# A hybrid decoder layer on one core: the merge gates' products moved to a stage of their own with seven block products for eight, and the tiles of the attention's scores re-cut

## The chip, the core and the metric

One core of a Trainium2 chip runs the whole layer in one launch. The time is the device time of one execution in microseconds; less is better. Three runs of the kernel before took 1770.57 to 1776.94 us, with a median of 1774.29.

## What is computed

2048 tokens of width 1024, float32. With `h = x @ W_in + b_in` cut into columns:

```python
y_a = mla_attention(c_q, c_kv, k_pe, ...) * silu(z_a)      # 8 heads, 96-wide q and k, 64-wide v, causal
y_b = u_gelu * mixed(layer_norm(gelu(v))) * silu(z_b)      # 128x128 mixing per group of 64 columns
merged = sigmoid(g_a) * (y_a @ w_oa) + sigmoid(g_b) * (y_b @ w_ob)
out = layer_norm(alpha * x + merged @ w_out)
```

`g_a` and `g_b` are the merge gates: 1024 columns of `h` each, so 2048 of the 4640 columns of `W_in`. The columns `z_a`, `u` and `z_b` are 512 each.

## The kernel before

**Arithmetic.** Every float32 operand of a product is cut into a head `hi` and a rest `lo` (`split`, line 64: a copy on ScalarE, a subtraction on VectorE), and `mm3` (line 68) adds `hi*hi + hi*lo + lo*hi` in PSUM: three matmuls of up to 512 columns.

**Stages.** Stage 1 (lines 141 to 359) computes q, k and v of the attention and writes them to DRAM. Stage 2 (lines 361 to 491) computes v of the gating unit and mixes it: `gelu_v` per token tile, `mix` per chunk of 512 tokens, whose results `mo` go to DRAM (line 475). `gates()` (lines 493 to 568) makes the columns `u`, `z_b`, `z_a` and both merge gates: 28 blocks of 128 columns, for the chunks of x in two pairs, (0, 1) and then (2, 3), since two chunks of x fit on chip as (hi, lo). One block of one chunk is a `group`: 8 steps of three matmuls in one PSUM bank (pool `p3G`, two banks), then a bias on VectorE (line 522), or for the merge gates a tanh on ScalarE (line 518), and a store by GpSimd's queue (lines 519, 548). Line 571 runs 48 steps of this generator, next to the end of stage 2; the others fill the attention.

**The attention** (lines 574 to 767) handles 64 blocks (head, 256 queries). A block has three kinds of steps on TensorE. `score` (line 619) multiplies 128 queries with up to 512 keys into one bank of `ps_s` (four banks); VectorE adds the mask and takes the maximum (lines 631 to 639), and once the whole row has its maximum, ScalarE takes the exponentials (line 642). `turn` (line 648) transposes 2 x 2 blocks of probabilities into `ps_t` (one bank), which ScalarE and VectorE split into `ph` and `pl`. `product` (line 670) multiplies these with V.

**The order on TensorE** is written out ahead of time by a planner (lines 694 to 754) that keeps a clock `now` and assumes lags: a score tile's bank comes free `LAG_S` after the row plus `LAG_E` a tile, `ph` and `pl` are there `LAG_H` and `LAG_T` after a turn, the output bank `LAG_O` after a block. In each round it first pays back credit with one filler step of the gates, then tries a product, a turn, a score, and if none is due takes a filler step too. Every attention step adds `FILL` times its cost to the credit; a filler step is reckoned at 648 ns. What is left of the filler runs behind the attention (line 765). `tc.keep_in_program_order` fixes this order where `keep[0]` is set; elsewhere a scheduler orders each engine's instructions.

**The last stage** (lines 774 to 873) reads gates, attention and mixed v back, multiplies with `w_oa`, `w_ob` and `w_out`, and normalises.

SBUF pools opened in a stage's `ExitStack` are given back at its end, and the next stage's tiles lie in the same memory.

## Time and profile before

| what | before |
|---|---|
| median of three runs | 1774.29 us |
| lowest, highest run | 1770.57, 1776.94 us |
| profiled execution, first to last instruction | 1775.5 us |
| TensorE busy | 1731.4 us, 98% |
| VectorE busy | 1094.2 us, 62% |
| ScalarE busy | 754.6 us, 43% |
| GpSimd busy | 134.3 us, 8% |
| mean granted clock of TensorE | 0.992 |

The profiled execution's own time is known as its span, 1775.5 us, which lies within the runs. Times in the trace count from the first instruction. A matmul's row gives its start and how long it is in the pipeline; the next one starts before it ends, so what a matmul occupies is the distance between starts. Engines are PE (TensorE), PEld (its weight loads), DVE (VectorE), ACT (ScalarE), POOL (GpSimd) and SP (the queue of most DMAs).

### The profile page before, as it was taken

The page shows a single profiled execution, that of the slowest core. Times are in us where ns is not written, and L with a number is a line of the kernel's source. Part 1 is how long each engine was busy: PE and PEld are TensorE (multiplying, and loading weights), DVE is VectorE, ACT ScalarE, POOL GpSimd, SP SyncE. Part 2 cuts the span into 40 slices and gives each one's busy share as a digit, 9 for nine tenths or more (in the row PEclk, how much of TensorE's full clock was granted, in tenths as well). Part 3 has the DMA queues.
Part 4 walks back from the last instruction along what each step waited for, and adds up shares of the span by engine and source line. Part 5 has one row for each costly group of instructions (what it writes and reads, how often), then busy time and mean ns, then how long its engine had stood idle before and what let it go on. Part 6 is the DMA issues. An engine that isn't in the chain of part 4 may idle for free.

```text
span 1775.5 us, 25048 instructions
## 1 busy us (share of the span) xinstructions
PE 1731.4 (98%) x9249; PEld 1484.1 (84%) x9249; DVE 1094.2 (62%) x2209; ACT 754.6 (43%) x1708; POOL 134.3 (8%) x231
## 2 busy tenths in 40 slices
PE   7999999899999999999999999999999999999998
PEld 7999887788888888888788888888888877888886
DVE  6765686476664555444776666654445478777664
ACT  6533442255544454545655445544544341303020
POOL 0000011100000100000100000100001000000000
PEclk9999999999999999999999999999999999999999
DMA  6564851631321422422713212321123886657341
GB/s 220 194 196 160 276 170 38 181 99 49 101 72 66 140 68 66 119 68 75 215 62 89 76 55 81 122 72 59 60 66 120 283 270 225 215 197 215 120 131 72
DMA packets 111100, 229.06 MB, mean 129 GB/s; under 512 B 13120, under 2 KB 41920, under 8 KB 108608
## 3 DMA queue, kind: packets, MB, share of 16 engines
q1 hardware_dynamic: 99968, 193.88, 34.9%
q0 software_dynamic: 11008, 33.57, 5.4%
q8 instruction: 73, 1.20, 0.3%
q14 instruction: 51, 0.42, 0.1%
HBM read 155.50 MB, written 71.89 MB: 128 GB/s over the span
## 4 chain that ended last, share of the span: by engine, by line
PE 45%; issue 41%; DMA 5%; POOL 4%; DVE 3%; ACT 2%; SPq 0%; POOLq 0%; DVEq 0%; ACTq 0%
PE po L86 11%; PE psg L86 9%; PE psa L86 4%; PE psl L86 4%; PE pb L86 4%; PE pa L86 4%; PE pss L86 3%; PE pt L658 2%; POOL gd L519 2%; DMA wost<-in_w_out_dram 1%; PE psq L86 1%; POOL otd L686 1%; DMA xst<-in_xT_dram 1%; DMA mxd<-mo 1%; PE psr L86 1%
## 5 line engine op out<-in xcount | busy, mean ns | idle before, releaser
L86 PE MATMUL psg<-xh,fwh 128*128 128x512 f32 x896 | 375.3, 419 | 4.9 <-DVE fo L522 4.9
L66 DVE TENSOR_TENSOR pl<-pt,ph 128x512 fp32r<-128x512 f32 (+2 forms) x352 | 199.7, 567 | 287.2 <-ACT ph L65 285.5
L86 PE MATMUL psg<-xl,fwh 128*128 128x512 f32 x896 | 354.5, 396 | 0.0
L86 PE MATMUL psg<-xh,fwl 128*128 128x512 f32 x896 | 354.1, 395 | 0.0
L65 ACT CAST ph<-pt 128x512 fp32r<-128x512 f32 (+2 forms) x352 | 172.0, 489 | 241.4 <-PE pt L658 208.8
L642 ACT ACTIVATE pr<-pss,nm 128x512 f32<-128x512 f32 (+2 forms) x320 | 198.0, 628 | 114.9 <-DVE nm L639 95.9
L86 PE MATMUL pss<-Kh,Q 96*128 96x512 f32 (+3 forms) x640 | 222.5, 377 | 12.9 <-DMA Q<-qrd 7.2
L86 PEld LDWEIGHTS psg<-xh,fwl 128*128 128x128 f32 x896 | 169.6, 189 | 38.4
L636 DVE TENSOR_REDUCE mx<-pss 128x1 f32<-128x384 f32 (+2 forms) x288 | 175.6, 619 | 29.4 <-PE pss L86 26.1
L86 PEld LDWEIGHTS psg<-xh,fwh 128*128 128x128 f32 x896 | 170.6, 190 | 25.6 <-issue 5.3
L86 PEld LDWEIGHTS psg<-xl,fwh 128*128 128x128 f32 x896 | 171.4, 191 | 20.7
L658 PE MATMUL pt<-ident,pr 128*128 128x128 f32 x1088 | 167.2, 274 | 0.0
L86 PEld LDWEIGHTS pss<-Kh,Q 96*128 96x128 f32 x640 | 119.3, 189 | 30.7 <-ACT pr L642 9.7
L658 PEld LDWEIGHTS pt<-ident,pr 128*128 128x128 f32 x1088 | 125.6, 141 | 5.8 <-ACT pr L642 0.4
L86 PEld LDWEIGHTS po<-ph,V 128*128 128x128 f32 x576 | 108.7, 189 | 26.0 <-ACT ph L65 3.2
L86 PE MATMUL pss<-Kl,Q 96*128 96x512 f32 (+2 forms) x320 | 115.9, 362 | 0.0
L86 PE MATMUL po<-pl,V 128*128 128x256 f32 x576 | 113.9, 279 | 0.2
L86 PE MATMUL po<-ph,V 128*128 128x256 f32 x576 | 112.8, 276 | 1.2 <-DVE o L685 0.7
L86 PEld LDWEIGHTS po<-pl,V 128*128 128x128 f32 x576 | 96.5, 190 | 11.3 <-DVE pl L66 1.2
L86 PE MATMUL po<-woh,mh 128*128 128x512 f32 x256 | 100.8, 394 | 1.2 <-ACT mh L65 1.2
L86 PE MATMUL po<-woh,ml 128*128 128x512 f32 x256 | 100.4, 393 | 0.0
L86 PE MATMUL po<-wol,mh 128*128 128x512 f32 x256 | 99.7, 390 | 0.0
(208 smaller groups left out, 2986.3 us busy)
## 6 DMA issues: line engine op xcount, KB each, us to landing
fst<-in_w_feat_dram SPq DMA_DIRECT2D x56, 512.0 KB, 3.7
gd<-fo POOLq DMA_DIRECT2D x96, 256.0 KB, 2.3
wabst<-in_w_ab_dram SPq DMA_DIRECT2D x32, 512.0 KB, 4.2
xst<-in_xT_dram SPq DMA_DIRECT2D x31, 512.0 KB, 4.9
kd<-e SPq DMA_DIRECT2D x16, 512.0 KB, 3.2
vd<-ve SPq DMA_DIRECT2D x16, 512.0 KB, 4.1
qnd<-e SPq DMA_DIRECT2D x16, 512.0 KB, 4.7
Q<-qnd SPq DMA_DIRECT2D x64, 128.0 KB, 2.9
```

The source lines that it names most:

```text
L65: act.copy(hi, src)
L66: dve.tensor_tensor(lo, src, hi.bitcast(F32), op=ALU.subtract)
L86: inorder(pe.matmul(*args, **kw))
L519: pool.dma_start(gd[c][m], o)
L636: dve.tensor_reduce(self.mx[:, i:i + 1], ps[:, :n], axis=AX.X, op=ALU.max)
L642: act.activation(pr[:, k0:k0 + ne], pe_[:, :ne], AF.Exp, bias=self.nm, accum_out=ls[:, self.h, 2 * self.qc + j, e:e + 1])
L658: inorder(pe.transpose(pt[:, i, j * P:(j + 1) * P], self.pr[j][:, (k + i) * P:(k + i + 1) * P], ident))
L686: pool.dma_start(otd[self.qc // 2][self.h * DV:(self.h + 1) * DV, self.qc % 2 * 256:(self.qc % 2 + 1) * 256], o2)
```

## The change

The merge gates leave `gates()`. A new stage between stage 2 and the first gate steps computes them in 16 rounds, each for two chunks of tokens and one block of `g_a` columns together with one of `g_b` (a quad: four outputs of 128 x 512, with the 1024 input columns in two halves). A quad has seven products of 12 matmuls (`product`) instead of eight, on sums and differences of the weight quarters (`columns`, on GpSimd, cut by `split`) and of the x quarters (`sums`: x loaded again as float32, added on GpSimd, split). The sums of x are made once for each pair of chunks, during the first quad for (0, 1), and product by product during the eighth for (2, 3). The next quad's weights are cut during a quad. TensorE's order is fixed in this stage.

x is now held in halves of four k tiles, so that half a chunk's memory can hold the sums. `gates()` keeps 12 blocks, takes chunks (2, 3) first, has one PSUM bank instead of two, and subtracts its weights' heads on GpSimd instead of VectorE. In the attention a score tile has up to 1024 keys in two banks, with two such tiles; a row of up to eight key blocks is one tile, a longer one two. Turned probabilities have two banks. The planner's lags and `FILL` are set anew.

```diff
-MT_ORDER = [m for f in range(4) for m in (MT_U + f, MT_ZB + f, MT_ZA + f)] + list(range(MT_GA, MT))
-LAG_S, LAG_E, LAG_H, LAG_T, LAG_O = 1500.0, 700.0, 1500.0, 2100.0, 1500.0
-FILL = 1.19       # time of the gates' products per time of the attention's
+MT_ORDER = [m for f in range(4) for m in (MT_U + f, MT_ZB + f, MT_ZA + f)]
+LAG_S, LAG_E, LAG_H, LAG_T, LAG_O = 2000.0, 400.0, 1500.0, 2100.0, 1500.0
+LAG_G = 1200.0
+FILL = 0.46
...
+    with ExitStack() as ph:
+        xq = ph.enter_context(tc.tile_pool(name="p2s", bufs=1))
+        xr = ph.enter_context(tc.tile_pool(name="p2r", bufs=1))
+        dw = ph.enter_context(tc.tile_pool(name="p2W", bufs=7))
+        dt = ph.enter_context(tc.tile_pool(name="p2d", bufs=2))
+        ps_d = ph.enter_context(tc.tile_pool(name="p2D", bufs=1, space=PSUM))
+        keep[0] = True
+        QUADS = [(MT_GA + m, MT_GB + m) for m in range(8)]
...
+        b, d = (xp.tile([P, 4, C], F32, tag=f"x0{e}", name=f"xsum{e}") for e in range(2))
+
+        def sums(c0, c1, have):
...
+            def combine(out, a, b, op):
+                for j in range(4):
+                    pool.tensor_tensor(out[:, j, :], a[:, j, :], b[:, j, :], op=op)
+
+            a = raw(c0, 0)
...
+            c = raw(c1, 1)
...
+            raw(c1, 0, b)
+            combine(d, b, c, ALU.add)
+            s = new(1)
+            halves(d, *s)
+            yield s
+            combine(b, a, b, ALU.subtract)
+            s = new(3)
+            halves(b, *s)
+            yield s
+            combine(d, d, a, ALU.subtract)
+            s = new(2)
+            halves(d, *s)
+            yield s
+            a = raw(c0, 1)
...
+            combine(d, a, d, ALU.subtract)
+            s = new(4)
+            halves(d, *s)
+            yield s
+
+        def columns(m1, m2):
...
+            pool.tensor_tensor(t1, w12, w11, op=ALU.subtract)
+            pool.tensor_tensor(t2, w22, t1, op=ALU.subtract)
+            pool.tensor_tensor(t4, w21, t2, op=ALU.subtract)
+            pool.tensor_tensor(w12, w22, w12, op=ALU.subtract)
+            for v in (w11, t4, t1, w12, t2, w21, w22):
+                yield cut(v)
+
+        def product(ps, w, x, more=False):
+            for j in range(4):
+                for i, (a, b) in enumerate(((0, 0), (0, 1), (1, 0))):
+                    mm(ps, w[a][:, j, :], x[b][:, j, :], start=not more and j == 0 and i == 0,
+                       stop=j == 3 and i == 2, skip_group_check=more)
...
+            A = ps_d.tile([P, C], F32, tag="A", bufs=2, name="dA")
+            step(0, A)
+            u2 = dt.tile([P, C], F32, tag="u2", name="du2")
+            act.copy(u2, A)
...
+            step(4, B6)
+            dve.tensor_tensor(u2, B6, u2, op=ALU.add)
+            u3 = dt.tile([P, C], F32, tag="u3", name="du3")
+            dve.tensor_tensor(u3, B7, u2, op=ALU.add)
+            out_of(B5, c1, m2, u3)
+            step(5, A, True)
+            out_of(A, c0, m1)
+            out_of(E, c1, m1, u3)
+            step(6, B5, True)
+            out_of(B5, c0, m2, u2)
...
+    psg_cm = tc.tile_pool(name="p3G", bufs=1, space=PSUM, side="right")
...
             for k in range(0, KD, 4):
-                split(st[:, k:k + 4, :], wh[:, k:k + 4, :], wl[:, k:k + 4, :])
+                act.copy(wh[:, k:k + 4, :], st[:, k:k + 4, :])
+                pool.tensor_tensor(wl[:, k:k + 4, :], st[:, k:k + 4, :], wh[:, k:k + 4, :].bitcast(F32),
+                                   op=ALU.subtract)
...
-        for cs2 in ((0, 1), (2, 3)):
+        for cs2 in ((2, 3), (0, 1)):
...
-        ps_s = ph.enter_context(tc.tile_pool(name="p3S", bufs=4, space=PSUM))
-        ps_t = ph.enter_context(tc.tile_pool(name="p3T", bufs=1, space=PSUM))
+        ps_s = ph.enter_context(tc.tile_pool(name="p3S", bufs=2, space=PSUM))
+        ps_t = ph.enter_context(tc.tile_pool(name="p3T", bufs=2, space=PSUM))
...
+                    n0 = nb if nb <= 8 else max(6, -(-nb // 2))
+                    self.todo.append((j, 0, 0, n0 * P, n0 == nb))
+                    if n0 < nb:
+                        self.todo.append((j, 1, n0 * P, (nb - n0) * P, True))
...
-            if credit > 0.0:
+            if credit > 0.0 and (nf % KD or g_free <= now):
...
-                    for _ in row:
-                        act_free += LAG_E
+                    for n in row:
+                        act_free += LAG_E + 0.9 * n
...
+                nf += 1
+                g_free = now + cost + LAG_G
```

## Rows read from the trace of the kernel before

**Rows 1.** The page: one engine's or all engines' busy time (share), instructions.

```profile
PE 1731.4 (98%) x9249; PEld 1484.1 (84%) x9249; DVE 1094.2 (62%) x2209; ACT 754.6 (43%) x1708; POOL 134.3 (8%) x231
```

**Rows 2.** Windows by stage; busy us per engine (count), granted clock, DMA share, GB/s.

```profile
0.00:307.00 307.00, 294.24 (x1783) 258.74 (x1784) 209.75 (x552) 133.92 (x287) 27.91 (x48) 0.99 0.54 180
307.00:353.60 46.60, 41.26 (x188) 33.14 (x187) 20.92 (x38) 10.90 (x20) 6.19 (x11) 0.93 0.62 183
353.60:1366.00 1012.40, 998.02 (x5544) 866.65 (x5542) 589.05 (x1203) 519.79 (x1282) 80.34 (x147) 0.99 0.28 85
1366.00:1411.70 45.70, 45.70 (x204) 37.91 (x204) 23.27 (x34) 15.83 (x25) 4.88 (x9) 1.00 0.86 294
1411.70:1775.50 363.80, 352.19 (x1537) 287.69 (x1536) 251.19 (x382) 74.17 (x95) 15.02 (x17) 0.99 0.56 181
```

**Rows 3.** Windows, gate products alone (tile psg), in the attention.

```profile
353.60:1366.00 1012.40, 647.55 (x2344) 417.15 (x2343) 32.19 (x43) 38.02 (x55) 0.99 0.28 85
```

**Rows 4.** Timeline of TensorE behind the attention; 43 rows between; start us, us.

```profile
1374.81 0.39 PE L86 MATMUL psg<-xh,fwl 128*128 128x512 f32 x1
...
1384.79 0.39 PE L86 MATMUL psg<-xl,fwh 128*128 128x512 f32 x1
```

**Rows 5.** Timeline of TensorE in the attention.

```profile
1200.47 0.39 PE L86 MATMUL psg<-xh,fwh 128*128 128x512 f32 x1
...
1201.17 0.40 PE L86 MATMUL po<-ph,V 128*128 128x256 f32 x2
```

**Rows 6.** Groups by form, VectorE, 353.6 to 1366 us; busy us, mean ns.

```profile
L636 DVE TENSOR_REDUCE mx<-pss 128x1 f32<-128x512 f32 x152 | 103.9, 686 | 16.0 <-PE pss L86 13.9
L636 DVE TENSOR_REDUCE mx<-pss 128x1 f32<-128x384 f32 x128 | 70.4, 552 | 13.4 <-PE pss L86 12.2
L66 DVE TENSOR_TENSOR fwl<-fst,fwh 128x512 fp32r<-128x512 f32 x98 | 65.9, 687 | 24.5 <-ACT fwh L65 24.1
...
L522 DVE TENSOR_SCALAR fo<-psg,bft 128x512 f32<-128x512 f32 x43 | 32.2, 749 | 13.9 <-PE psg L86 13.0
```

**Rows 7.** Timeline of TensorE at the end of stage 2.

```profile
314.85 0.28 PE L86 MATMUL psm<-vh,wsl 128*128 128x256 f32 x1
...
319.65 1.14 PE L472 MATMUL ptu<-ident,um 128*128 128x128 f32 x8
```

**Rows 8.** Groups by form, ScalarE, 353.6 to 1366 us.

```profile
L65 ACT CAST fwh<-fst 128x512 fp32r<-128x512 f32 x98 | 58.5, 623 | 36.4 <-PE psg L86 36.0 <-DMA fst<-in_w_feat_dram 0.4
L518 ACT ACTIVATE fo<-psg,bfh 128x512 f32<-128x512 f32 x55 | 38.0, 691 | 14.4 <-PE psg L86 14.4
```

**Rows 9.** Timeline of all engines, 326 to 341 us; idle before, releaser.

```profile
337.94 0.48 DVE L691 MEMSET ls<- 128x512 f32 x1 [8.47 <-DMA mxd<-mo]
```

**Rows 10.** Windows of 10 and of 5 us.

```profile
10.00:20.00 10.00, 10.00 (x77) 10.00 (x76) 8.19 (x13) 7.35 (x13) 0.00 (x0) 1.00 0.98 366
340.00:345.00 5.00, 5.00 (x12) 3.87 (x13) 4.54 (x7) 2.01 (x4) 0.54 (x1) 0.50 0.97 294
```

**Rows 11.** Groups by form, GpSimd, whole span.

```profile
L519 POOL DMA_DIRECT2D gd<-fo x64 | 35.5, 555 | 359.5 <-ACT fo L518 334.3 <-ACT ph L65 25.3
...
L427 POOL TENSOR_SCALAR_AFFINE_SELECT wsst<-wsst 128x1024 f32<-128x1024 f32 x1 | 1.1, 1099 | 20.5 <-DMA wsst<-in_wsT_dram 20.5
L106 POOL TENSOR_SCALAR_AFFINE_SELECT ident<-ident 128x128 f32<-128x128 f32 x1 | 0.3, 292 | 0.6 <-DVE ident L105 0.6
```

**Rows 12.** The page, DMA issues: count, KB each, median us to landing.

```profile
gd<-fo POOLq DMA_DIRECT2D x96, 256.0 KB, 2.3
...
xst<-in_xT_dram SPq DMA_DIRECT2D x31, 512.0 KB, 4.9
```

**Rows 13.** Timeline of TensorE around the hole at 335 us.

```profile
334.52 0.39 PE L86 MATMUL psg<-xh,fwl 128*128 128x512 f32 x1
339.77 0.76 PE L86 MATMUL psg<-xh,fwh 128*128 128x512 f32 x1 [4.87 <-DVE fo L522]
...
345.86 0.40 PE L86 MATMUL psg<-xh,fwl 128*128 128x512 f32 x1
```

More of the change, by code (lines that the diff above doesn't have):

```diff
@@ L124, in hybrid_layer_kernel, with x_half, xk, x_pieces @@
     xt = {}
-    def x_pieces(c):
-        hi = xp.tile([P, KD, C], F32R, tag="xh", name=f"xh{c}")
-        lo = xp.tile([P, KD, C], F32R, tag="xl", name=f"xl{c}")
-        xt[c] = (hi, lo)
-        for k in range(0, KD, 2):
+    def x_half(c, f):
+        xt.setdefault(c, {})[f] = tuple(xp.tile([P, 4, C], F32R, tag=f"x{f}{e}", name=f"x{f}{e}{c}") for e in range(2))
+    def xk(c, k):
+        return tuple(x[:, k % 4, :] for x in xt[c][k // 4])
+    def x_pieces(c, halves=(0, 1)):
+        for f in halves:
+            x_half(c, f)
+        for k in range(4 * halves[0], 4 * halves[-1] + 4, 2):
             st = xs.tile([P, 2, C], F32, tag="st", name="xst")
@@ L245, in latent @@
     def latent(c, ts):
-        xh, xl = xt[c]
         pss = {}
@@ L257, in latent @@
             cs = slice(h2 * 272, (h2 + 1) * 272)
-            mm3(pss[t, h2], (xh[:, k, tk], xl[:, k, tk]),
+            mm3(pss[t, h2], tuple(x[:, tk] for x in xk(c, k)),
                 (wlh[:, k, cs], wll[:, k, cs]), k == 0, k == KD - 1)
@@ L493, in gates @@
+    fw_cm = tc.tile_pool(name="fw", bufs=2, side="right")
+    fw = fw_cm.__enter__()
+    psg_cm = tc.tile_pool(name="p3G", bufs=1, space=PSUM, side="right")
+    ps_g = psg_cm.__enter__()
     def gates():
@@ L624, in score @@
                     self.nm = sm.tile([P, 1], F32, tag="nm", name="nm")
-                ps = ps_s.tile([P, 512], F32, tag="s", name="pss")
-                ks = slice(k0, k0 + n)
-                mm(ps[:, :n], Qh, self.Kh[:, ks], start=True, stop=False)
-                mm(ps[:, :n], Qh, self.Kl[:, ks], start=False, stop=False)
-                mm(ps[:, :n], Ql, self.Kh[:, ks], start=False, stop=True)
+                ps = ps_s.tile([P, 1024], F32, tag="s", name="pss")
+                for c0 in range(0, n, 512):
+                    cs = slice(c0, min(n, c0 + 512))
+                    ks = slice(k0 + c0, k0 + cs.stop)
+                    mm(ps[:, cs], Qh, self.Kh[:, ks], start=True, stop=False)
+                    mm(ps[:, cs], Qh, self.Kl[:, ks], start=False, stop=False)
+                    mm(ps[:, cs], Ql, self.Kh[:, ks], start=False, stop=True)
                 if last:
@@ L645, in score @@
                     self.sts = []
-                return 3 * n / 2.4, last
+                return 3 * n / 2.4, last, n
             def turn(self):
@@ L701, in hybrid_layer_kernel @@
         now = credit = 0.0
-        banks = [0.0] * 4
+        banks = [0.0] * 2
         row, turned = [], []
-        t_ready = o_free = act_free = 0.0
+        o_free = act_free = g_free = 0.0
+        t_ready = [0.0] * 2
+        nf = 48
         def block(n):
@@ L727, in hybrid_layer_kernel @@
                     o_free = now + cost + LAG_O
-            elif ti < si and ti <= vi + 1 and done_s[ti] <= now and t_ready <= now and len(turned) < 2:
+            elif ti < si and ti <= vi + 1 and done_s[ti] <= now and t_ready[0] <= now and len(turned) < 2:
                 cost = blocks[ti].turn()
-                t_ready = now + cost + LAG_T
-                turned.append([now + cost + LAG_H, t_ready])
+                t_ready = t_ready[1:] + [now + cost + LAG_T]
+                turned.append([now + cost + LAG_H, t_ready[-1]])
                 if blocks[ti].kt == blocks[ti].nk:
@@ L734, in hybrid_layer_kernel @@
             elif si < len(order) and si <= ti + 1 and banks and banks[0] <= now:
-                cost, last = blocks[si].score()
+                cost, last, n = blocks[si].score()
                 banks.pop(0)
-                row.append(now + cost)
+                row.append(n)
                 if last:
                     act_free = max(now + cost + LAG_S, act_free)
-                    for _ in row:
-                        act_free += LAG_E
+                    for n in row:
+                        act_free += LAG_E + 0.9 * n
                         banks.append(act_free)
```

119 lines of the change are left out of this document (94 added, 25 removed).

## The prediction

> **What bounds the kernel now.** I read the page first, then busy time by stage, then single instructions. On the page TensorE is busy for 1731.4 of 1775.5 us, VectorE for 1094 and ScalarE for 755 [rows 1]: TensorE is the bound, so what counts is its work and its holes. By stage [rows 2], the attention with its filler takes 1012.4 us and TensorE idles 14.4 of them; behind it 45.7 us are gate products alone. In the attention 2344 of the 2688 gate matmuls run [rows 3], which is 781 steps of three.
>
> Busy time counts the tail of a pipelined matmul, so I go by starts. Alone, 45 gate matmuls start within 9.98 us: 44 gaps of 0.2268 us [rows 4]. Between steps of the attention three take 0.70 us, 0.233 each [rows 5]. So the filler holds 2344 × 0.233 = 546 us of the 1012.4, and the attention's own work and its waits hold 466.
>
> **The change, in order of time.** The sum is made against the span of 1775.5 us; it lies 1.2 us above the median of the runs, which I take off at the end.
>
> *Products.* The merge gates take 16 × 4 × 24 = 1536 matmuls before and 16 × 84 = 1344 after. 1344 × 0.2268 = 304.8 us; the 192 that go are worth 43.5. The eviction, seven weight splits and five sums of a quad are some 12 × 0.69 = 8.3 us on VectorE [rows 6] under 19 us of matmuls: covered.
>
> *Entry.* Today the first filler steps run among the end of stage 2. After, the weights and sums of the new stage lie in SBUF that stage 2's pools give back. The last mixing matmul starts at 314.85, the last turns end near 320.8 [rows 7]; then a cast of 0.62 [rows 8] and a subtraction of 0.69 [rows 6]: first product at 322, 15 us after 307. Bounds: 315 if only the mixing is waited for; 338 if the buffers lie under the last stored tile, since today VectorE's memset of `ls` waits until 337.9 for just that store [rows 9].
>
> *First quad.* Products 0 and 1 use x as it stands, the third needs x loaded again, added and split. Three loads of 1 MB at the highest rate seen, 366 GB/s, down to 294 [rows 10] take 8.6 to 10.7 us: the first sum can start at 326, from 315. The trace has no two-input operation over a whole tile on GpSimd. Its nearest rows, affine_select over 1024 and 128 columns [rows 11], give 0.18 us plus 0.9 ns a column, 0.64 us for 512; reading two sources twice that slope, 1.10. I take 1.10, as there are two sources; the bounds are 0.64 and 1.4, the last being two whole instructions. Sixteen such adds stand in a chain, with a load of 4.9 us [rows 12] ahead of the last four: 326 + 17.6 + 4.9 + 2 for the last splits and products = 350.5, against 341 without a wait. The next quad's four weight operations share the queue: I take 12 us, bounds 2 and 20.
>
> *Half clock.* Today a hole of 4.9 us behind a `fo` eviction is followed by 14 matmuls in 6.1 us instead of 3.2, at a granted clock of 0.50, the 1.2 GHz level [rows 10, 13]: 2.9 us more. The first quad's waits should bring that once: 3 us.
>
> *Turn and quads.* In the eighth quad VectorE has 28 splits of x besides its usual 12 operations, 27.6 us in 19; but product i of the ninth needs only item i, so I take 3 us, bounds 0 and 9. In each quad the seventh product waits for three VectorE sums behind the fifth, 2.1 us and perhaps a split of 0.69, while the sixth covers 2.7: 0.3 each, 5 us; bounds 0 and 16.
>
> *Leaving.* The next gate weights can be split only when the stage's last tiles are out: sum 0.69, tanh 0.69 [rows 8], store 2.3 [rows 12], issue 0.56 [rows 11], cast 0.62: 5 us, and the half clock 3 more: 8; bounds 0 and 11.
>
> *48 first steps.* 144 × 0.2268 = 32.7. With one bank for the filler each of six groups must be emptied before the next starts: VectorE's 0.75 [rows 6], 0.17 for the tail and some signalling, near 1 us: 38.7 in all.
>
> *Attention.* Following the written order by its own rules, before it places 781 filler steps, as the trace shows, and 372 of these because credit forces them. After it places 315 of 336, 314 of them because nothing else is due; 21 stay for the end. So the filler is 945 × 0.233 = 220 us, and with the own 466 that is 686. At 24 of the 39 group ends the next group follows before its single bank is empty, 24 us at most; I charge 15, since the attention's own chain goes on meanwhile. The rest: 128 fewer maxima save about 0.15 us each, the part that does not scale between the 512 and 384 column forms [rows 6], and the weight subtraction leaves VectorE (65.9 us [rows 6]). VectorE's 589 falls to near 500 us, of 706: 71% where it was 58%. A score tile of 1024 columns holds it for some 1.2 us, and what is behind it is late by that. I charge 5 for this; bounds for the whole attention 670 and 770. Total 706. The second bank for turned probabilities lets a turn start earlier, which helps only if turns are late now; the idle of 14.4 us bounds that.
>
> *Tail and the rest.* 21 steps are 63 × 0.2268 = 14.3, with three emptied banks 17. Stages 1 and the last stay: 307 and 363.8.
>
> **Sum:** 307 + 15 + 304.8 + 12 + 3 + 3 + 5 + 8 + 38.7 + 706 + 17 + 363.8 = 1783.3; less 1.2 it is 1782. The products that go give 43.5; the joints and the thinner cover take more than that.
>
> **The rivals.**
> 1. *The joints are covered, faster.* Entry 12, first quad 7, half clock 3, turn 0, quads 2, leaving 4, first steps 34, attention 688, tail 15: 1740.6, so 1739. For it: the sums' loads may be issued ahead, each bound of a joint reaches near 0, and lags of 2000 and 400 + 0.9 ns a column leave the scores more time than the old ones. Against it: the `ls` wait shows what a reused buffer costs. It wins if the attention holds 690 and the entry product starts before 320. Chance 0.33.
> 2. *VectorE's queue sets the attention.* No forced filler stands between a row's steps any more; if each of the 128 rows of scores is late by 0.35 us beyond the forecast, that is 45 us: 1827. For it: 314 of 315 fillers stand where nothing is due, so a late step is a hole. Against it: TensorE's real steps are slower than the planner's (0.233 against 0.216 us), which widens each lag. It decides from 0.2 us a row. Chance 0.19.
> 3. *GpSimd and VectorE exclude each other.* In the first quad VectorE splits what GpSimd adds; if each of the 24 GpSimd operations there first waits out one split of 0.69 us, the chain grows by 16 us: 1798. Against it: splits and sums alternate anyway. Chance 0.05. The Trainium skill, "SBUF — State Buffer", section "Who interferes with whom", says that a VectorE instruction with two SBUF inputs and a GpSimd instruction that reads SBUF lock each other out for the whole instruction. No row here shows both at work, so the trace neither supports nor denies it.
>
> That the stage's quads would be bound by something other than TensorE is excluded by 8.3 us of VectorE in 19.
>
> A price that only a page states: the Trainium skill, "GPSIMD Engine Reference", section "Performance versus the Vector engine", puts a two-input f32 operation at 1.96 times VectorE's time; an estimate by it is 1.35 us for 512 columns, and the first quad would wait some 17 us instead of 12, the sum 1787. The rows reach to 1.4 by themselves.
>
> **How the numbers follow.** About 0.3% (5 us) can be told from no change. The forecast, 1765 to 1800, has 0.43, of which 0.04 lies below 1769 and 0.14 within 0.3%. Faster: 0.33 + 0.04 = 0.37; same 0.14; slower 0.25 + 0.19 + 0.05 = 0.49. Rival 1 spreads down to some 1720, rival 2 up to 1850; leaving a tenth out on each side gives 1734 to 1828. The forecast's own range is 1765 to 1800.
>
> **What would show it.** In the profile after: 1344 matmuls in a stretch of near 330 us with TensorE idle in the first quad; a granted clock of 0.5 there and behind the stage; `psg` behind `fo` waits at group ends; the attention at 700 to 715 us with 945 gate matmuls. An attention over 735 with `pss` or `po` waiting for VectorE means rival 2; a stage under 320 us and an attention under 690 mean rival 1; GpSimd adds over 1.4 us in the first quad mean rival 3.

## The result, and the profile after

The changed kernel takes 1883.5 us (median of 4 runs, 1880.1 to 1884.4) against 1775.6 us (4 runs, 1770.6 to 1776.9): 1.0615 times as long, interval 1.0596 to 1.0635. The prediction was 1782, with a range of its own of 1765 to 1800 and 1828 as the upper end of the wider one. It had the side right, by 8 us and with a chance of 0.49, and the size wrong. The kernel before was timed again beside each set of experiments, with medians of 1770.9 to 1774.6 us; each ratio is against that, and the distance between two versions from different sets is known to some 5 us.

The page's busy times of the changed kernel, to be read against [rows 1]:

```profile
PE 1730.9 (92%) x9105; PEld 1462.5 (78%) x9105; DVE 1217.7 (65%) x2177; ACT 782.4 (42%) x1564; POOL 337.3 (18%) x375
```

TensorE is busy for 0.5 us less than before, although it has 144 matmuls fewer (192 of the merge gates go, and the re-cut scores have 1008 where they had 960), and its share falls from 98% to 92%: the engine waits more, and works part of the time at a lower clock. By stage of the changed kernel (window, its length, then busy time and count of TensorE, weight loads, VectorE, ScalarE, GpSimd; granted clock, DMA share, GB/s), against [rows 2]:

```profile
307.00:330.90 23.90, 12.38 (x61) 9.26 (x60) 9.46 (x21) 6.31 (x12) 4.97 (x9) 0.72 0.34 124
330.90:695.90 365.00, 324.49 (x1344) 258.10 (x1344) 202.41 (x239) 141.77 (x238) 166.35 (x155) 0.93 0.33 114
695.90:702.10 6.20, 0.07 (x1) 0.00 (x0) 1.03 (x2) 1.40 (x3) 0.54 (x1) 0.82 0.75 220
702.10:743.20 41.10, 36.42 (x144) 27.97 (x145) 11.95 (x16) 7.99 (x14) 11.90 (x11) 0.94 0.66 192
743.20:1484.90 741.70, 694.21 (x4196) 607.71 (x4195) 510.11 (x938) 410.61 (x911) 103.54 (x129) 0.98 0.25 71
1484.90:1504.80 19.90, 16.48 (x63) 12.49 (x62) 12.90 (x21) 5.29 (x9) 2.23 (x4) 0.91 0.82 259
1504.80:1881.00 376.20, 354.42 (x1537) 288.71 (x1536) 262.35 (x397) 77.97 (x99) 15.22 (x17) 0.98 0.60 194
```

The rows are, in order: the entry up to the first block product, the seven-product stage, the hole behind it, the 48 first steps, the attention, the tail, the last stage. The boundary at 307 is taken over from before. TensorE idles for 40.5 us of the seven-product stage (365.0 − 324.49), and for 47.5 us of the attention, where it had 14.4. What TensorE waited for over the whole span (engine and tile, what ended the wait: us in all, times, longest):

```profile
PE psg L87 <- DVE fo L687: 32.5, 29, 2.6
PE dD L87 <- DVE do L599: 20.7, 2, 17.7
PE pb L87 <- ACT wabh L66: 12.6, 4, 10.4
PE dD L87 <- ACT s L66: 11.0, 2, 9.2
PE pss L87 <- DMA Q<-qrd: 10.4, 4, 4.6
PE pss L87 <- ACT pr L809: 6.8, 7, 1.5
```

The first row is the group ends of the filler's single bank, the second and fourth are the new stage's, the third lies ahead of the last stage. Of before, [rows 13] show one such wait.

Each term of the prediction's sum against the profile, on the profiled execution's span of 1881.0 us:

| term | forecast | measured | miss |
|---|---|---|---|
| stage 1 | 307 | 307 | 0 |
| entry | 15 | 23.9 | +8.9 |
| stage of seven products (304.8 + 12 + 3 + 3 + 5) | 327.8 | 365.0 | +37.2 |
| leaving it | 8 | 6.2 | −1.8 |
| 48 first steps | 38.7 | 41.1 | +2.4 |
| attention with thin filler | 706 | 741.7 | +35.7 |
| tail | 17 | 19.9 | +2.9 |
| last stage | 363.8 | 376.2 | +12.4 |
| sum | 1783.3 | 1881.0 | +97.7 |

### The profile page after: what moved, and what is told of

Read it like the earlier page. It is cut to its first block, busy times and chain, and to the rows that moved or that the text cites. A ratio compares the mean times of both kernels' runs of the same rounds, so it can differ in the third digit from the quotient of the medians.

```text
span 1881.0 us, 24943 instructions
## 1 busy us (share of the span) xinstructions
PE 1730.9 (92%) x9105; PEld 1462.5 (78%) x9105; DVE 1217.7 (65%) x2177; ACT 782.4 (42%) x1564; POOL 337.3 (18%) x375
## 4 chain that ended last, share of the span: by engine, by line
PE 68%; DVE 10%; DMA 7%; issue 5%; ACT 5%; POOL 4%; SPq 1%; DVEq 0%; ACTq 0%; POOLq 0%
PE po L87 14%; PE psg L87 10%; PE pss L87 9%; PE pt L825 5%; PE dD L87 4%; PE pb L87 4%; PE pa L87 4%; PE psl L87 4%; PE dA L87 3%; PE psa L87 3%; DVE pl L67 2%; PE dE L87 2%; PE dB L87 2%; PE dC L87 2%; POOL xsum L526 2%
## 5 line engine op out<-in xcount | busy, mean ns | idle before, releaser
L87 PE MATMUL psg<-x,fwh 128*128 128x512 f32 x768 | 256.3, 415 | 40.2 <-DVE fo L687 32.5
L87 PE MATMUL pss<-Kh,Q 96*128 96x512 f32 (+3 forms) x672 | 217.7, 370 | 17.8 <-DMA Q<-qrd 10.4
L809 ACT ACTIVATE pr<-pss,nm 128x768 f32<-128x768 f32 (+5 forms) x192 | 166.8, 871 | 125.7 <-DVE nm L806 82.4
L87 PEld LDWEIGHTS psg<-x,fwh 128*128 128x128 f32 x768 | 131.8, 193 | 66.1 <-DVE fo L687 39.7
L803 DVE TENSOR_REDUCE mx<-pss 128x1 f32<-128x768 f32 (+5 forms) x128 | 126.6, 989 | 46.3 <-PE pss L87 44.7
L87 PE MATMUL psg<-x,fwl 128*128 128x512 f32 x384 | 153.8, 401 | 0.2 <-POOL fwl L673 0.2
L87 PE MATMUL dD<-s,dwh 128*128 128x512 f32 x256 | 88.9, 427 | 39.2 <-DVE do L599 20.7
L87 PE MATMUL pss<-Kl,Q 96*128 96x512 f32 (+1 forms) x336 | 119.9, 357 | 0.0
L67 DVE TENSOR_TENSOR dwl<-dst,dwh 128x512 fp32r<-128x512 f32 x64 | 68.9, 1079 | 76.1 <-ACT dwh L66 73.4
L87 PE MATMUL psl<-wlh,x 128*128 128x272 f32 x512 | 103.3, 297 | 5.9 <-ACT wlh L66 5.9
L853 POOL DMA_DIRECT2D otd<-o x64 | 34.9, 545 | 392.7 <-DVE o L852 269.7
```

Source lines behind the costliest of these rows:

```text
L67: dve.tensor_tensor(lo, src, hi.bitcast(F32), op=ALU.subtract)
L87: inorder(pe.matmul(*args, **kw))
L803: dve.tensor_reduce(self.mx[:, i:i + 1], ps[:, :n], axis=AX.X, op=ALU.max)
L809: act.activation(pr[:, k0:k0 + ne], pe_[:, :ne], AF.Exp, bias=self.nm, accum_out=ls[:, self.h, 2 * self.qc + j, e:e + 1])
L853: pool.dma_start(otd[self.qc // 2][self.h * DV:(self.h + 1) * DV, self.qc % 2 * 256:(self.qc % 2 + 1) * 256], o2)
```

## Experiments

All were timed beside the kernel before, in four runs or more, but the kernels of experiments 5 and 13, which ran once each. The edits are against the changed kernel unless the text says otherwise.

**1. A second bank for the filler.** To hold the eight PSUM banks, it is taken from the turned probabilities. Two filler banks, two turned ones and score tiles of two banks don't fit together, so that was not tried.

```diff
-psg_cm = tc.tile_pool(name="p3G", bufs=1, ...)
+psg_cm = tc.tile_pool(name="p3G", bufs=2, ...)
-ps_t = ph.enter_context(tc.tile_pool(name="p3T", bufs=2, space=PSUM))
+ps_t = ph.enter_context(tc.tile_pool(name="p3T", bufs=1, space=PSUM))
-t_ready = [0.0] * 2
+t_ready = [0.0]
```

> The changed kernel with two banks for the gate steps again and one bank for turned probabilities (the planner keeps one ready time). Theory 1, the single bank is what the attention lost most by: its waits behind the bias eviction (24.6 us in the attention, 4.5 in the first steps, 3.4 behind) go, TensorE's idle time in the attention falls from 47.5 to about 20 us, and the kernel takes 1845 to 1860 us. Rival, the attention is held by its own chains and these waits only stand where it would wait anyway: under 10 us gained, 1873 us or more.

Measured: 2062.96 us (1.1653, interval 1.1622 to 1.1684); neither reading had that. TensorE's waits in this kernel:

```profile
PE po L87 <- ACT ph L66: 71.6, 97, 1.7
PE pb L87 <- ACT wabh L66: 31.7, 5, 28.8
```

The value products now wait for the casts of turned probabilities, and the filler ran out at 1225.6 us while the attention lasted until 1674.5. With one turned bank the written order finds more rounds in which nothing is due than there are filler steps. So the one-bank turn of before lives on thick filler, and the second turned bank is what lets the changed kernel do with 40% of it (947 of 2344 matmuls).

**2. The splits of x in the eighth quad are written behind the eviction's sums.** At the turn from the first two column blocks to the other two, VectorE's queue holds the coming sums' splits ahead of the eviction. Part of the edit is shown; the rest has VectorE keep this order:

```diff
-                if turn:
+                if turn and i < 2:
                     xc2.append(next(xg2))
...
             out_of(B5, c1, m2, u3)
+            items(1)
             step(5, A, True)
             out_of(A, c0, m1)
             out_of(E, c1, m1, u3)
+            items(1)
             step(6, B5, True)
             out_of(B5, c0, m2, u2)
+            items(3)
...
```

> The changed kernel; in the eighth quad the splits of the third x quarter and of those behind it are written after the eviction sums, and VectorE keeps that order. Theory 1, the hole of 17.7 us there is VectorE's queue (splits that wait for GpSimd's sums stand ahead of the eviction that TensorE waits for): the hole shrinks to 5 us or less and the kernel gains 12 to 18 us, 1863 to 1870. Rival, VectorE and GpSimd simply have that much to do there: the wait moves to the products of the ninth quad and less than 6 us is gained.

Measured: 1873.4 us (1.0574, 1.0557 to 1.0592), 10 us below the changed kernel by the medians and 7 by the ratios: between the two readings. The eighth quad falls from 39.7 to 21.6 us, but the ninth grows from 19.6 to 34.3: most of the wait moved there, as the rival had it.

**3. All sums of the stage on VectorE.**

```diff
-                    pool.tensor_tensor(out[:, j, :], a[:, j, :], b[:, j, :], op=op)
+                    dve.tensor_tensor(out[:, j, :], a[:, j, :], b[:, j, :], op=op)
-            pool.tensor_tensor(t1, w12, w11, op=ALU.subtract)
+            dve.tensor_tensor(t1, w12, w11, op=ALU.subtract)
(and the three weight sums below it)
```

> The changed kernel with all sums of x and of weights on VectorE, so GpSimd does no tile arithmetic in the stage. Theory 1, GpSimd and VectorE hold each other up there: the splits fall back from 0.79 to 1.18 us to 0.69, a sum takes 0.69 instead of 1.33 to 1.85, the first quad's waits shrink by about 10 us, and the stage takes 345 to 355 us instead of 365. Rival, the durations come from something else (memory, the DMAs): splits stay at 1 us or more and, with 128 more operations on VectorE, the stage takes 370 us or more.

Measured: 1861.56 us (1.0508, 1.0485 to 1.053), 22 us faster than the changed kernel by the medians and 19 by the ratios, although VectorE has more to do; the stage falls from 365.0 to 347.8 us, as theory 1 had it. First the changed kernel's VectorE groups by form in its stage (busy us, mean ns of one | idle before):

```profile
L67 DVE TENSOR_TENSOR dwl<-dst,dwh 128x512 fp32r<-128x512 f32 x64 | 68.9, 1079 | 76.1 <-ACT dwh L66 73.4 <-PE dE L87 2.7
...
L67 DVE TENSOR_TENSOR s<-xsum,s 128x512 fp32r<-128x512 f32 x32 | 33.3, 1067 | 11.2 <-ACT s L66 9.7
L599 DVE TENSOR_TENSOR do<-dD,du 128x512 f32<-128x512 f32 x32 | 22.0, 689 | 32.7 <-DMA gd<-do 32.2
```

and the splits here:

```profile
L67 DVE TENSOR_TENSOR dwl<-dst,dwh 128x512 fp32r<-128x512 f32 x64 | 44.1, 691 | 63.6 <-ACT dwh L66 63.5
...
L67 DVE TENSOR_TENSOR s<-xsum,s 128x512 fp32r<-128x512 f32 x32 | 20.1, 691 | 0.0
```

The same split of 512 columns takes 1079 ns on average beside GpSimd's sums and 691 without them. The average hides how: by the shortest, the median and the longest, in ns, half of these weight splits in the changed kernel are not slowed at all, and a few stand for several us:

```profile
L67 DVE TENSOR_TENSOR dwl<-dst,dwh x64: 678/693/5676, 330.9 to 677.1; 128x512 fp32r<-128x512 f32 x64
```

The longest began at 385.94 us, and GpSimd ran four adds without a gap, to 391.06, before it ended. The eviction sums, whose one input lies in PSUM, take 689 in the changed kernel all the same. GpSimd's groups in the changed kernel's stage show the other side, 1848 ns where the queue meets VectorE's splits most and 1349 where it does so less:

```profile
L526 POOL TENSOR_TENSOR xsum<-xsum,xraw 128x512 f32<-128x512 f32 x16 | 29.3, 1848 | 16.0 <-PE dE L87 9.9 <-DVE s L67 6.1
...
L584 POOL TENSOR_TENSOR dst<-dst 128x512 f32<-128x512 f32 x15 | 20.2, 1349 | 0.0
```

The edit does two things at once: it ends the overlap, and it makes an add shorter, 0.69 us on VectorE where GpSimd's shortest took 1.26. What either is worth by itself was not tried.

**4. A plain stage of eight products** (1536 matmuls, no sums, the rest as changed):

```diff
-            for v in (w11, t4, t1, w12, t2, w21, w22):
-                yield cut(v)
...
+            for k in range(KD):
+                mm3(ps, tuple(v[:, k, :] for v in w), xk(c, k), k == 0, k == KD - 1)
```

> The changed kernel with a plain stage in place of the seven products: the 16 merge gate blocks for each chunk as eight block products, 1536 matmuls, no sums of x or of weights, the chunks of x exchanged in pieces between products. Theory 1, the scheme costs more than the 43.5 us of matmuls that it saves: the stage takes 350 to 358 us (348 us of matmuls), and the kernel 1866 to 1876, faster than the changed one. Rival, what the stage loses is its place (entry, cold clock, leaving), whatever it computes: 385 us or more for the stage, over 1895 for the kernel.

Measured: 1855.36 us (1.0478, 1.0453 to 1.0504), 28 us faster than seven products by the medians and 24 by the ratios. Theory 1 had the stage right and the kernel 11 us too slow. Windows of its stage and of its attention:

```profile
323.00:675.90 352.90, 352.90 (x1539) 289.52 (x1538) 50.53 (x75) 85.28 (x143) 40.19 (x69) 1.00 0.32 111
714.40:1455.50 741.10, 692.89 (x4196) 606.65 (x4195) 509.97 (x938) 410.19 (x911) 102.80 (x128) 0.99 0.25 71
```

The stage runs without a gap, 352.9 us for 1536 matmuls, and its attention costs what the changed kernel's costs. This kernel has as many gate matmuls as the one before, and its profiled span is 74.8 us longer (1850.3 − 1775.5): that is the price of everything in the change but the scheme, the products out of the attention's cover and the attention's re-cut together. The scheme by itself costs the other 30.7 (1881.0 − 1850.3): it saves 43.5 in matmuls and loses 74 at the entry, in the quads and behind them. By the ratios the two parts are 85 and 24 us. No run has the products moved and the attention as it was, so lost cover and re-cut are told apart only by argument, from experiment 5.

**5. The attention without any filler, in both kernels.** The steps that the written order places among the attention are not done there but behind it; the order of the rest stays. The same line goes in the kernel before.

```diff
             else:
                 cost = 648.0
                 credit -= cost
-                next(fill, None)
                 nf += 1
```

> The changed kernel with no filler step among the attention: all that is left of the gates behind it, the order of the attention's own steps unchanged. Theory 1, the attention with thin filler runs at the pace of its own chain (scores, maximum, exponentials, turn, split, product) and the filler lies in its holes: alone it takes 600 to 700 us, against 741.7 with 945 gate matmuls, which are 214 us by themselves. Rival, TensorE's work sets it: 466 us of own work and waits, at most 540.

> The kernel before with no filler among the attention, the rest of the gates behind it. Theory 1, its chain with one bank for turned probabilities is slower still than the changed one: 750 to 900 us for the attention alone, so that 546 us of filler in 1012 had covered most of it. Rival, it takes 466 us or little more, as the sum of the prediction had it: at most 540.

Measured: the changed kernel 2087.1 us, the one before 2146.9, one run each; what counts is the attention. Changed kernel:

```profile
743.80:1436.20 692.40, 549.38 (x3255) 476.66 (x3254) 421.91 (x804) 354.19 (x803) 36.87 (x66) 0.92 0.18 48
```

```profile
PE pss L87 <- ACT pr L809: 84.5, 72, 2.7
...
PE po L87 <- ACT ph L66: 17.7, 53, 0.7
```

The kernel before:

```profile
349.00:1202.90 853.90, 660.96 (x3203) 516.30 (x3201) 441.59 (x965) 391.07 (x1059) 33.40 (x64) 0.86 0.15 40
```

```profile
PE po L86 <- ACT ph L65: 105.1, 148, 1.3
PE po L86 <- DVE pl L66: 40.4, 152, 0.9
PE pss L86 <- ACT pr L642: 30.9, 36, 1.5
```

Without filler the attention takes 692.4 and 853.9 us, not the 466 of the prediction. Both show how small the real gain of thinner filler must be: 947 gate matmuls, some 215 us, lengthen the changed attention by 49 (741.7 − 692.4), and 2344 of them, 532 us, lengthen the other by 158 (1012.4 − 853.9). Without filler the evictions and weight splits of the gates are gone from the attention too (VectorE 421.9 us busy instead of 510.1), so the 49 and 158 hold the filler's work on all engines. The re-cut attention is the shorter one by 161 us when nothing covers it; that speaks against the re-cut as the cause of the loss under thin filler, though it is no run of it.

**6. Every seventh filler step held back for the end** (45 of them):

```diff
-                next(fill, None)
-                nf += 1
+                skipped += 1
+                if skipped % 7 != 3:
+                    next(fill, None)
+                    nf += 1
```

> The changed kernel with every seventh filler step of the attention left out of it, 45 in all, and done behind it. Theory 1, the holes are there whether filled or not: the attention gets under 12 us shorter though 31 us of matmuls leave it, and the kernel 5 to 20 us slower, 1875 to 1895, with the 13 us hole at the start of the last stage gone. Rival, TensorE's work sets the attention: it falls by about 31 us, the tail grows by as much, and the last stage's hole goes: 1862 to 1868.

Measured: 1897.07 us (1.0699, 1.0679 to 1.072). 135 matmuls, 31 us, leave the attention, and it gives back 12.1 (741.7 to 729.6), far nearer to theory 1 than to the rival; the kernel is 2 us above theory 1's range. The hole of 10.4 us at the start of the last stage goes, and TensorE's longest wait for `wabh` is 3.4 us. What is behind the filler's end falls from 376.2 to 366.8 us, but 23 of that stage's matmuls, some 5 us, now stand among the filler, so the longer tail brings some 4 us and not the whole hole.

**7. The attention's part of the change alone, in the kernel before** (score tiles of two banks, two turned banks, one filler bank, the new lags):

```diff
-LAG_S, LAG_E, LAG_H, LAG_T, LAG_O = 1500.0, 700.0, 1500.0, 2100.0, 1500.0
+LAG_S, LAG_E, LAG_H, LAG_T, LAG_O = 2000.0, 400.0, 1500.0, 2100.0, 1500.0
-... name="p3S", bufs=4 ... name="p3T", bufs=1 ... name="p3G", bufs=2 ...
+... name="p3S", bufs=2 ... name="p3T", bufs=2 ... name="p3G", bufs=1 ...
```

> The kernel before with the attention's part of the change alone: score tiles of two banks, two banks for turned probabilities, one for the filler, the planner's new lags and its wait for the filler's bank; the merge gates stay in the filler and FILL stays 1.19. Theory 1, thick filler covers the chain, so this edit by itself costs next to nothing: 1765 to 1795. Rival, the single filler bank costs its near 1 us at most of the 112 group ends whatever the cover: 1830 or more.

Measured: 1849.46 us (1.043, 1.0411 to 1.0449). That is the rival's reading: this edit costs 76 us under thick filler. The group ends of the filler's one bank appear, with 48.7 of them:

```profile
PE psg L87 <- ACT fo L519: 31.6, 26, 2.4
PE psg L87 <- DVE fo L523: 17.1, 16, 5.7
```

**8. The score tiles and lags alone, in the kernel before** (one turned bank and two filler banks stay):

```diff
-... name="p3S", bufs=4 ...   (the lags as in 7)
+... name="p3S", bufs=2 ...
```

> The kernel before with the score tiles of two banks and their lags alone; one bank for turned probabilities and two for the filler as before. Theory 1, under thick filler the tiles neither cost nor give much: 1765 to 1785. Rival, the tile of 1024 columns holds VectorE and ScalarE so long that turns and products are late: 1800 or more.

Measured: 1780.32 us (1.0043, 1.0026 to 1.006). As theory 1 had it, the score tiles by themselves cost little under thick filler, 7.5 us.

**9. One filler bank alone, in the kernel before:**

```diff
-psg_cm = tc.tile_pool(name="p3G", bufs=2, ...)
+psg_cm = tc.tile_pool(name="p3G", bufs=1, ...)
```

> The kernel before with one PSUM bank for the gate groups instead of two and nothing else; one bank stays unused. Theory 1, the single bank is most of what the attention's part of the change cost by itself (1849 against 1773): near 0.5 us at each of 112 group ends, 1815 to 1850. Rival, the larger score tiles or their lags cost it: under 1795 here.

Measured: 1904.84 us (1.0747, 1.0729 to 1.0765), more than any reading had:

```profile
PE psg L86 <- ACT fo L518: 68.5, 51, 3.6
PE psg L86 <- DVE fo L522: 27.1, 35, 6.1
```

Here the written order does not know that the bank must be emptied, so thick filler meets it 86 times. These waits are 95.6 of the 132 us lost (1904.8 against 1772.8 beside it).

**10. The changed kernel without the wait for that bank.** The eviction reads x in SBUF in place of the finished sum, so u, z_b and z_a are left out of the result.

```diff
-            dve.tensor_scalar(o, ps, bft[:, m:m + 1], None, op0=ALU.add)
+            dve.tensor_scalar(o, xk(c, 0)[0].bitcast(F32), bft[:, m:m + 1], None, op0=ALU.add)
```

> The changed kernel with the eviction of a gate group reading x in SBUF instead of the group's PSUM bank: the gates' values u, z_b and z_a are left out of the output, every instruction count stays, and the single bank is free for the next group at once. Theory 1, the waits for the single bank come on top of the chain: the 32.5 us of waits behind the eviction go from first steps, attention and tail, and some 10 hidden in weight loads, so 1840 to 1855. Rival, the chain of the attention takes back what the bank gives: under 12 us gained, 1869 or more.

Measured: 1875.91 us (1.0588, 1.0568 to 1.0608), 7.6 us below the changed kernel by the medians and 5 by the ratios, whose intervals overlap. All 32.5 us of waits on `fo` are gone, and the attention takes what it took:

```profile
736.10:1478.40 742.30, 698.50 (x4196) 611.23 (x4194) 486.64 (x927) 409.27 (x907) 104.61 (x131) 0.96 0.25 72
```

742.3 us, idle for 43.8, now elsewhere, at a granted clock of 0.96 where it was 0.98. That is the rival's number, but its reason is not shown, since the edit makes waits of its own. An eviction no longer waits for its matmuls, so it runs early, and VectorE's queue then stands behind a store that must free an output tile. TensorE waits for VectorE behind it, 10 us in one place; in the changed kernel the same wait is 0.2 us:

```profile
1120.24 0.49 DVE L687 TENSOR_SCALAR fo<-x,bft 128x512 f32<-128x512 f32 x1 [6.16 <-DMA gd<-fo]
```

```profile
PE po L87 <- DVE o L852: 10.0, 1, 10.0
```

A further 5.9 us are a second wait for gate weights, where the changed kernel has one and that ahead of its first steps. So what the single bank costs under thin filler stays open.

**11. Experiments 2 and 3 together:**

```diff
-                    pool.tensor_tensor(out[:, j, :], a[:, j, :], b[:, j, :], op=op)
+                    dve.tensor_tensor(out[:, j, :], a[:, j, :], b[:, j, :], op=op)
-                if turn:
+                if turn and i < 2:
...
```

> The changed kernel with both mends of the new stage: sums on VectorE, and in the eighth quad the splits behind the eviction sums in VectorE's order. Theory 1, the two add up, as one removes the mutual hold-up and the other the queueing: the stage takes 335 to 342 us and the kernel 1848 to 1858. Rival, once the sums are on VectorE the queue there is full either way: no better than 1861, as with the sums alone.

Measured: 1859.24 us (1.0487, 1.0465 to 1.0509), no different from experiment 3 alone by more than the runs scatter. In the profiled executions the stage takes 343 us, some 5 less than in experiment 3 and 1 above theory 1's range; in experiment 2 the order of the splits took 4.3 us off the stage. So in the stage the two seem to add up.

**12. One memset moved in the kernel before.** [rows 9] showed `ls` waiting for a store on VectorE, in front of a filler eviction and the hole of [rows 13].

```diff
-        dve.memset(ls, 0.0)
+        pool.memset(ls, 0.0)
```

> The kernel before with the memset of the row sums on GpSimd instead of VectorE, nothing else. Theory: the hole of 4.9 us that the prediction read there and the half clock behind it are VectorE's queue behind that memset, which waits for a store; both go, 4.9 + 2.9 = 7.8 us, and the kernel takes 1763 to 1768, faster than both kernels. Rival: the bias eviction waits for something else behind it, or GpSimd's stores get late in its place: under 3 us.

Measured: 1770.44 us (median of 12 runs) against 1774.59 (17 runs), 0.9979 with an interval of 0.9968 to 0.999: faster than both kernels. GpSimd waits for the store now, and stage 2's end keeps its clock (the window had 0.93 before):

```profile
335.79 0.53 POOL L691 MEMSET ls<- 128x512 f32 x1 [8.17 <-DMA mxd<-mo]
```

```profile
307.00:353.60 46.60, 45.21 (x223) 36.78 (x222) 26.44 (x51) 16.54 (x33) 7.53 (x14) 1.00 0.67 199
```

The first score starts at 345.9 instead of 353.6 us, 7.7 earlier: the hole's 4.9 and the half clock's 2.9 us. Some four of these reach the end (1.8 to 5.7 by the interval), so the kernel missed theory's 1763 to 1768; where the rest goes was not traced.

**13. Which link of the attention's chain?** The changed kernel without filler, once with every exponential done twice, once with every subtraction for the rest of the turned probabilities done twice.

```diff
+                        act.activation(pr[:, k0:k0 + ne], ...)   (the block a second time)
...
+                    dve.tensor_tensor(pl_, pt, ph_.bitcast(F32), op=ALU.subtract)   (a second time)
```

> The changed kernel without filler among the attention, every exponential written twice (192 more activations with their sums, about 200 us more for ScalarE). If the chain of a score tile's buffer (score, maximum, exponentials, next score) sets the 692 us, the attention grows by 130 to 200 us. If the turns do (transposes, split, product), it grows by less than 80 us.

> The changed kernel without filler among the attention, every subtraction behind a turn written twice (288 turns, about 185 us more for VectorE). If the score buffers set the 692 us, the attention grows by less than 80 us, VectorE having room; if the turns or VectorE as a whole do, by 130 to 190 us.

Measured: the attention takes 908.9 us with the exponentials doubled and 878.0 with the subtraction, 217 and 186 more than the 692.4 of experiment 5. The added ScalarE work is some 208 us, the added VectorE work some 190. First with the exponentials, then with the subtraction doubled (window, then waits):

```profile
742.20:1651.10 908.90, 645.68 (x3254) 560.53 (x3253) 430.80 (x804) 522.22 (x1188) 37.12 (x66) 0.81 0.14 37
PE pss L87 <- ACT pr L811: 202.7, 76, 4.2
```

```profile
743.80:1621.80 878.00, 645.36 (x3256) 550.34 (x3255) 589.76 (x1156) 358.32 (x803) 37.12 (x66) 0.83 0.14 38
PE pss L87 <- ACT pr L809: 127.2, 68, 3.3
PE po L87 <- DVE pl L838: 51.6, 60, 1.8
```

Each grows by more than the 80 us that was allowed for a link off the path. TensorE's idle time grows by 120 us with the one and by 90 with the other; the other 96 us in each are TensorE's own busy time, 549.4 before, at granted clocks of 0.81 and 0.83 instead of 0.92. So no "either–or" holds: in this written order both links lie on the path, one behind the other. Which of them one would have to shorten first stays open.

## Why the prediction was wrong

Two terms hold 73 of the 98 us, the attention and the stage of seven products; the last stage and the entry hold 21 more.

**The step that failed** in the attention is "the filler holds 2344 × 0.233 = 546 us of the 1012.4, and the attention's own work and its waits hold 466", carried over as "with the own 466 that is 686". The 466 is TensorE's work under thick cover, and no time in which the attention can be done. The changed attention without filler takes 692.4 us: 549.4 busy and 143.0 idle (experiment 5). Of the 694.2 busy in the changed kernel, the 947 gate matmuls are 947 × 0.2268 = 214.8, so the attention's own share is 479.4; without filler the same work is busy for 70 us more. The granted clock, 0.92 where it was 0.98, can account for some 40 of the 70 (an estimate from the two windows: 0.08 of 692.4 us against 0.02 of 741.7). The rest is not explained by a run; part of it may be the tails of pipelined matmuls, which filler behind them hides. Adding the filler fills 95.5 us of idle (143.0 − 47.5) and takes these 70 back: 214.8 − 95.5 − 70.0 = 49.3, and 692.4 + 49.3 is the measured 741.7. For the kernel before the same sum is 531.6 − 178.5 − 194.6 = 158.5 on top of 853.9. So filler in this kernel mostly sits in time that would be lost anyway, and counting each of its matmuls at 0.233 us is wrong: 1397 leave, 325 us by that price, and the filler's part of the attention falls by 109 (158.5 − 49.3).

That the term missed by no more than 35.7 us is luck in part. The attention fell from 1012.4 to 741.7 us because the re-cut shortens it by another 161 where nothing covers it (853.9 to 692.4), and the prediction gave the re-cut no such gain: "the idle of 14.4 us bounds that". Idle time under thick filler bounds nothing. In the kernel before without filler the products wait 145.5 us for the turned probabilities (`po` for `ph` and `pl` in experiment 5), in the changed one 25.5 (there the scores' wait for the exponentials is the longer one, 84.5 against 30.9).

Against the forecast's own parts, TensorE is busy for 22.6 more than the 671.6 that lay in it (466 − 14.4 + 220), and idle for 13.1 more than its 34.4.

**The stage of seven products, +37.2.** The step that failed is "8.3 us of VectorE in 19", with GpSimd's sums beside it at their undisturbed time. The products themselves were right: the quads that nothing disturbs start 19.4 to 19.6 us apart, against 84 × 0.2268 = 19.05, and the charge of 0.3 a quad for the seventh product was about what is seen. Three joints were not. The first quad took 48.4 us, 29 over, not 12 plus 3; the eighth 39.7, 20.6 over, not 3; the fifteenth 24.1, 5 over, not foreseen. Of the 60.2 us that the stage takes beyond 304.8, TensorE is idle for 40.5; the other 19.7 are matmuls at a slower pace, with a mean granted clock of 0.71 in the first quad, where "once: 3 us" was charged. The turn in the changed kernel, VectorE's timeline, then a row each of GpSimd's and ScalarE's, and TensorE's (start, length, engine, line, what; in brackets the idle time before it and what ended it):

```profile
518.06 5.25 DVE L67 TENSOR_TENSOR s<-xsum,s 128x512 fp32r<-128x512 f32 x4 [1.81 <-ACT s L66]
523.22 0.68 DVE L642 TENSOR_TENSOR du<-dB,du 128x512 f32<-128x512 f32 x1
...
527.95 0.68 DVE L644 TENSOR_TENSOR du<-dC,du 128x512 f32<-128x512 f32 x1
...
529.63 0.68 DVE L599 TENSOR_TENSOR do<-dD,du 128x512 f32<-128x512 f32 x1
530.23 5.19 DVE L67 TENSOR_TENSOR x<-xraw,x 128x512 fp32r<-128x512 f32 x3
```

```profile
510.91 6.46 POOL L526 TENSOR_TENSOR xsum<-xsum,xraw 128x512 f32<-128x512 f32 x1 [6.06 <-DVE s L67]
526.15 0.62 ACT L66 CAST x<-xraw 128x512 fp32r<-128x512 f32 x1 [3.57 <-DMA xraw<-in_xT_dram]
```

```profile
530.36 1.22 PE L87 MATMUL dD<-s,dwh 128*128 128x512 f32 x2 [17.72 <-DVE do L599]
...
535.65 0.82 PE L87 MATMUL dA<-x,dwh 128*128 128x512 f32 x2
```

The first of four sums on GpSimd takes 6.46 us: VectorE runs nine splits without a gap until 516.25, and it ends 1.1 us behind them. The other three take turns with VectorE's next splits and last 1.26 to 1.71 us, the splits up to 1.53 where experiment 3 had 0.69. Then x is loaded into the tile that these sums read, so the load starts when they end, and ScalarE's cast waits 3.57 us for it. VectorE works its queue in order, so the sums that empty the banks (`du` at 523.22 and 527.95, `do` at 529.63) wait behind all this, and TensorE waits 17.72 us for `do`. Behind the wait the product's last 12 matmuls take 5.3 us (530.36 to 535.65), 0.44 each where 0.2268 is the dense cadence: the half clock. The next block's splits of x in VectorE's queue, 5.19 us for three, are slower still, 1.15 to 2.43 each. That is rival 3's mechanism, which got a chance of 0.05 and 16 us in the first quad alone. Moving the sums to VectorE gave some 20 us back, the overlap and the shorter adds together (experiment 3). The argument against that rival, that splits and sums alternate anyway, is refuted by these rows: where they alternate both get longer, and where VectorE has splits that do not wait for GpSimd, the add waits for all of them.

The Trainium skill, "SBUF — State Buffer", section "Who interferes with whom", has the rule that rival 3 rested on: a VectorE instruction with two SBUF inputs and a GpSimd instruction that reads SBUF contend, one with at most a single SBUF input does not, outside the modes in which it uses both ports. The trace agrees: 1079 ns in the mean for the split of two SBUF tiles, 689 for the sums with one input in PSUM, 691 for the split once GpSimd does no tile arithmetic.

GpSimd's shortest add takes 1.26 us, above the 1.10 taken and inside its bounds of 0.64 and 1.4; the weight sums, which meet few splits, take 1.33 to 1.35 in the mean.

**The last stage, +12.4,** was costed at nothing. The filler's tail of 45.7 us [rows 2] had covered its loads; 19.9 do not:

```profile
1504.51 0.39 PE L87 MATMUL psg<-x,fwl 128*128 128x512 f32 x1
1515.30 0.79 PE L87 MATMUL pb<-ybh,wabh 128*128 128x512 f32 x1 [10.41 <-ACT wabh L66]
```

10.4 us of hole in front of the first output product, then the slower start. A longer tail removes the hole, so the lost cover is shown as its cause; but it brings back only some 4 of the 12.4 us (experiment 6), and where the rest would go is open. The term named no work that hid the loads, and so the loss of it was not seen.

**The entry, +8.9,** lies between its bounds: the first product started at 330.9, 322 was taken and 338 was the bound that `ls` gave. TensorE sat idle for 5.55 us of it until the weights' cast, and that cast waited for stage 2's last store of `mo`, the wait that the bound had named:

```profile
330.23 0.62 ACT L66 CAST dwh<-dst 128x512 fp32r<-128x512 f32 x1 [2.81 <-DMA mxd<-mo]
```

**Right:** the half clock's price of 2.9 us behind one such hole (experiment 12 gave back hole and clock together, 7.7), leaving the stage, the 48 first steps, the tail, and the single filler bank as a wait of some 24 us in the attention; whether it costs the 15 that were charged stays open (experiment 10). Of rival 2 one half holds: with nothing forced behind it, a late step is a hole, and the attention is over the 735 that it named. But the holes are not VectorE's: `pss` waits 6.8 us for ScalarE's exponentials and `po` 2.1 us for VectorE, and experiment 13 finds both engines' links on the path.

**What is lost to what,** by the profiled kernels: 74.8 us to all but the scheme, lost cover above all as argued from experiment 5, 45.5 of these in the attention (741.1 − 214.8 = 526.3 beside the gate matmuls, against 1012.4 − 531.6 = 480.8), 11.1 in the last stage, the rest at the joints; 30.7 to the scheme, whose saving of 43.5 is used up. Of the 30.7 some 20 go when the sums are on VectorE. No version of the changed kernel that was run came under the kernel before.

## What to carry to other kernels

Work that fills another stage's holes has no price per instruction: run the stage once without it, and count the difference. Before a filler is moved, list everything that runs under it, the loads of the stage behind included. Two-source sums on GpSimd are not free beside VectorE splits of SBUF tiles: cost both at their disturbed durations, or keep them on one engine. An edit that takes a wait away can let work run early and make a new wait, so read where the time went before the old wait is called free.

## What the runs showed of the hardware that was not expected

A 512-column f32 split on VectorE slowed from 691 to 1079 ns in the mean beside GpSimd sums. In turns the split took some 1.5 us and the sum 1.7, where 0.69 and 1.26 are the undisturbed times. Where one engine had a run of such instructions without a gap, one of the other's waited for the whole run: an add took 6.46 us beside nine splits, a split 5.68 beside four adds. Together the two engines did less than VectorE alone (365.0 us against 347.8 for the stage). Idle time costs TensorE twice: without filler, the same attention work was busy for 70 us longer in the changed kernel and 195 us in the one before, at granted clocks of 0.92 and 0.86 in place of 0.98 and 0.99, which can account for some 40 and 110 of these (estimates from the windows, as above). One PSUM bank fewer for the filler cost 132 us where the filler was thick and the written order did not allow for it (experiment 9).
